# Differential attention on one core: a unit's two softmax halves joined in the next unit, its transpositions two units and its products with the values three units behind the scores

## The chip, the cores and the metric

The kernel runs on one NeuronCore of a Trainium2 chip, as one program. The metric is the time of one execution on the device, in microseconds. Matmuls run on TensorE (PE, with PEld for its weight loads), elementwise work on VectorE (DVE), ScalarE (ACT) and GpSimd (POOL), and every DMA is issued by SyncE (SP).

## The reference, cut to what matters

The program is a two-layer backbone over 1024 latent tokens and 256 context tokens of width 1024. Layer 0 mixes tokens by differential attention, layer 1 by a state-space scan; a dense block follows each. The change lies in the attention of layer 0, which computes, for each of 8 heads and each query, two softmaxes over the same keys and one product with the values:

```python
def attend(q, k, v):
    s = jnp.einsum('bqhcd,bkhcd->bhcqk', q, k).astype(jnp.float32)
    p = jax.nn.softmax(s, axis=-1)
    w = p[:, :, 0] - lam * p[:, :, 1]
    o = jnp.einsum('bhqk,bkhe->bqhe', w.astype(v.dtype), v)
    return rmsnorm(o, subln_g) * (1.0 - lambda_init)
```

Latent queries see 256 context and 1024 latent keys (1280), context queries only the 256 context keys. The arithmetic keeps float32 accuracy: an operand is split into a high and a low part, and a product is three matmuls (`mm3`, lines 130 to 134).

## The kernel before, in words

The stage in question is `phase_b` (lines 617 to 922). Its unit of work is a pair (head h, unit u). Unit 0 of a head takes all 256 context queries against 256 keys; units 1 to 8 take 128 latent queries each against 1280 keys. 8 heads of 9 units make 72 passes n of one loop (line 806), and five more passes drain what is left. Within `self.manual()` the instructions of PE, DVE, ACT and POOL stay in the order in which the loop writes them, each engine in its own queue; only SP's DMAs are placed by the scheduler.

What a unit goes through:

- *Scores* (`scores`, lines 507 to 520): twelve matmuls into five PSUM banks that every unit uses, so the next unit's scores wait until the maxima have read them.
- *Maxima* (`maxima`, 523 to 533): DVE copies each half c to SBUF (`p[0]` from a ring of two buffers, `p[1]` always the same buffer), negated extremum on the way; 1280 columns each, L533 (L529 in unit 0).
- *Exponentials* (`exps`, 535 to 544): ACT, one for each half, with their sums; L543 (L540 in unit 0).
- *Combine* (`combine`, 546 to 554): DVE joins the halves, half 0 minus lambda times half 1, in `p[0]`: a reciprocal (L551), a small product (L552) and one over 1280 columns (L554).
- *Transpositions* (`w_part`, 556 to 569): ten on PE, in three parts of four, two and four, into bank 5, the second half of bank 6, and bank 7 (bank 5 again where the unit has a projection).
- *Evacuation* (`w_evac`, 571 to 581) into `wT`, as a high and a low part: the first part by ACT (L574) and DVE (L575), the others by ACT (L579) and POOL (L580, L581).
- *Products with the values* (`values`, 651 to 656): two units make a pair of 256 queries (unit 0 is a pair of its own), 30 matmuls into the first half of bank 6, six for unit 0. Then `pair_out` (L662 on ACT, L663 on POOL) and one unit later `pair_sums` (L669 on PE, into the first columns of bank 6, and L670).

Before the change the transpositions of unit n - 1 stand in pass n, and the products of a pair two passes behind its last unit: for pairs that end in units 0, 2, 4, 6 and 8 that is in units 2, 4, 6, 8 and the next head's 1.

Beside this the loop projects keys and queries of the next head. `AHEAD` (line 588) says which projection belongs to which unit: two in unit 0 (the first, of 256 columns, ahead of the scores), one each in units 2, 3, 5 and 7; the others' matmuls (24 each) are cut into three fills that stand behind the three parts of the transpositions. A projection collects in bank 7. It is evacuated at the end of its unit by L466 (ACT) and L467 (DVE), or L461 and L462 for a block of 256 columns, and `next_post` brings its further steps, one in the middle and one at the end of each unit: L472 (POOL), L475 (DVE, in the middle), the split of the result by L137 (ACT) and L138 (DVE, at the end of units 0, 2, 4 and 7). Heads from 1 on also normalize the head before: `norm_calc` (675 to 677, DVE), `norm_rows` (a transposition, L684), and for each pair `norm_load` (two DMAs into one buffer) and `norm_pair` (L694 on DVE, which waits for them, then L137 and L138 on the tile W). In head 7 the projections are replaced by ten output products (`wo_group`), one in each pass from 65 on, and the drain normalizes head 7 itself (`norm7`).

A unit's pass queues, in this order: scores, maxima, products with the values, then the three parts. `late` is set where the pass has products with the values of a full pair; there the evacuation of the first two parts comes behind the exponentials, since it overwrites what the products read. Line 863 to 868 hold this order:

```python
                    if front and part < 2:
                        self.exps(u, part, p, sm, s0, sn)
                    if front and part == 1:
                        self.combine(u, p, s0, sn)
                    if late and part == 1:
                        evac()
```

At the end of the pass stand `pair_out`, `next_post`, the projection's evacuation, splits of weights, `norm_calc` or `norm_rows`, and `norm_pair`.

Of the kernel before, what the change touches and what calls it, by code (L numbers as in the profile page):

```python
# [6 lines left out]
F32 = mybir.dt.float32  # L7
F32R = mybir.dt.float32r
# [5 lines left out]
KB = 256  # L14
# [56 lines left out]
class Prog:  # L71
# [544 lines left out]

    def phase_b(self):
        nc, mm = self.nc, self.nc.tensor.matmul
        p0 = Ring([self.view(self.F1, 5 * i, (1280,)) for i in range(2)])
        p1 = self.view(self.F1, 10, (1280,))  # L620
        self.wraw = Ring([self.view(self.F1, 15 + 2 * i, (512,)) for i in range(3)])
        o = self.fv(6, 256)
        sq = self.adat
        self.raw = Ring([self.wv(0, 1024)])
# [64 lines left out]
        def norm_load(h, pair):  # L689
            self.dma(nob, self.od[h, :, 256 * pair : 256 * pair + 256])  # L690
            self.dma(nrb, self.rsd[h, 2 * pair : 2 * pair + 2].rearrange("a b -> (a b)").partition_broadcast(128))
# [54 lines left out]
        def wsplit6(j):  # L746
            hi, lo = wregs[j]
            self.split(hi, lo, wraw6[j], nc.gpsimd)
            wt6.extend((hi[:, i], lo[:, i]) for i in range(2))

        def beside7(u):

            if u == 0:
                self.oT = self.hgroups()
                nc.vector.memset(ones, 1.0)
            if u < 2:
                wsplit6(u + 1)
            for g, k0, k1 in {0: ((2, 0, 6),), 1: ((0, 0, 3),), 2: ((0, 3, 6),), 3: ((1, 0, 3),), 4: ((1, 3, 6),)}.get(u, ()):
                c0 = (256, 768, 0)[g]
                for k in range(k0, k1):  # L760
                    for j in range(2):
                        self.dma(self.oT[g][j][:, k].bitcast(F32), self.on[k, j, :, c0 : c0 + self.G_TOK[g]])
# [17 lines left out]
        wo_order = [8, 9] + list(range(8))  # L780
# [5 lines left out]
        load_q(0, 1)  # L786
        load_v(0)
        units = [(h, u) for h in range(8) for u in range(9)]
        prev, todo, sums, post, tail, run7 = None, [], [], [], [], []
        split = self.proj_weights(1, 1)  # L790
        split(0)
        wts = {1: split(1)}
# [10 lines left out]
                self.w_evac(*ready.pop(0))  # L803

        with self.manual():
            for n in range(72 + 5):
                h, u = units[n] if n < 72 else (8, 9)
                front = n < 72
                groups = []
                pv = todo.pop(0)[1:] if todo and todo[0][0] == n else None  # L810
                late = pv and pv[1]
                parts = 3 if prev and prev[1] else 1 if prev else 0
                if front and n - 6 >= 9 and (n - 6) % 9 < 5 and (n - 6) // 9 < 7:
                    norm_load((n - 6) // 9 - 1, (n - 6) % 9)
                if h == 7 and u > 5:
                    load6(u)
                if front:
                    K = loaded[h, 'k', 0], loaded[h, 'k', 1]
                    pair = (u + 1) // 2
                    Q = loaded[h, pair]  # L820
                    s0 = hst[:, 0, h]
                    p, sn, sm = (p0.next(), p1), self.stat.next(), self.stat.next()
                    if u == 5 and h < 7:
                        load_v(h + 1)
                        load_k(h + 1, 0)
                    if u % 2 == 0 and u < 8 and (h, pair + 1) not in loaded:
                        load_q(h, pair + 1)
                    if h < 7:
                        groups = [self.proj_group(h + 1, *a, wts[a[0]]) for a in self.AHEAD.get(u, ())]
                    if len(groups) == 2:  # L830
                        for f in groups[0][0] + groups[0][1]:
                            f()
                    self.scores(u, Q, K)
                    if u == 8 and h < 7:
                        load_k(h + 1, 1)
                        load_q(h + 1, 0)
                        load_q(h + 1, 1)
                    self.maxima(u, p, sm)
                if front:
                    if h < 7:  # L840
                        if u == 0:
                            qsplit = self.proj_weights(h + 1, 0)
                        if u == 5 and h < 6:
                            ksplit = self.proj_weights(h + 2, 1)
                if 65 <= n < 75:
                    groups = [wo_group(wo_order[n - 65])]
                fills = [[], [], []]
                if h >= 7 and groups:
                    fills = [groups[0][0][i : i + 2] for i in (0, 2, 4)]
                elif groups:  # L850
                    fills = [groups[-1][0][i:j] for i, j in (((0, 4), (4, 8), (8, 8)) if u == 3 else ((0, 3), (3, 6), (6, 8)))]
                if pv:
                    values(*pv)
                for part in range(3):
                    if part < parts:
                        tb = pb[:, 256:512] if part == 1 else self.bank(7 if part == 2 and not groups else 5)
                        t = self.w_part(prev[1], prev[2], part, tb)
                        ready.append((*t, part == 0))
                    if not late or part == 2:
                        evac()  # L860
                    if part == 1:
                        next_post()
                    if front and part < 2:
                        self.exps(u, part, p, sm, s0, sn)
                    if front and part == 1:
                        self.combine(u, p, s0, sn)
                    if late and part == 1:
                        evac()
                    if part == 0:
                        todo7, run7 = run7, []  # L870
                        for f in todo7:
                            f.pop(0)()
                            if f:
                                run7.append(f)
                    if part == (2 if n < 73 else 0):
                        while sums and sums[0][0] <= n:
                            sums.pop(0)[1]()
                    for f in fills[part]:
                        f()
                if pv:  # L880
                    pair_out(*pv)
                    sums.append((n + 1, lambda a=pv: pair_sums(*a)))
                    if pv[0] == 7:
                        tail.append((n + 1, pv[1]))
                next_post()
                if groups:
                    rest = groups[-1][1]
                    rest[0]()
                    post += rest[1:]
                if h < 7 and u in (0, 2):  # L890
                    wts[0] = qsplit(u // 2)
                if h < 6 and u in (6, 7):
                    wk = ksplit(u - 6)
                if u == 8 and h < 6:
                    wts[1] = wk
                if front and u % 2 == 0:
                    todo.append((n + 2, h, pair))
                prev = (h, u, p[0]) if front else None
                if 0 < h < 8:
                    if u == 3:  # L900
                        newton = norm_calc(h - 1)
                    elif u == 4:
                        newton()
                    elif u == 5:
                        norm_rows(h - 1)
                if h < 8 and n - 6 >= 9 and (n - 6) % 9 < 5 and (n - 6) // 9 < 7:
                    norm_pair((n - 6) // 9 - 1, (n - 6) % 9)
                if n == 72:
                    self.raw = Ring([self.wv(8, 1024), self.wv(12, 1024)])
                    self.wo_raws = [self.wo_load(3, 0), self.wo_load(0, 1)]  # L910
                if n == 60:
                    wload6(0)
                if n == 62:
                    wload6(1)
                    wload6(2)
                    wsplit6(0)
                if h == 7:
                    beside7(u)
                    if u > 5:
                        norm6(u)  # L920
                if tail and tail[0][0] == n:
                    run7.append(list(norm7(tail.pop(0)[1])))
# [1270 lines left out]
    def run(self):  # L2193
        tc = self.tc
        pool = lambda name, **kw: tc.tile_pool(name=name, bufs=1, **kw)
        with pool("cst") as self.cst, pool("psp", space=bass.MemoryType.PSUM) as psp, \
# [23 lines left out]
            with pool("r0") as rp, pool("fc") as cp:  # L2220
# [6 lines left out]
                    self.raw = Ring([self.wv(4 * i, 1024) for i in range(4)] + [self.f0(24.5 + 4 * i, 1024) for i in range(4)])  # L2227
                    self.phase_v()
                with pool("r1") as rp, pool("f1") as fp:
                    self.R1, self.F1 = rp.tile([128, 20 * KB], F32R, name="R1"), fp.tile([128, 21 * KB], F32, name="F1")  # L2230
                    self.phase_b()
                for g in range(3):
                    for j in range(2):
# [72 lines left out]
```

## Time and profile before

| What | Value |
|---|---|
| Times of three runs, us | 2940.19, 2940.97, 2946.08 (median 2940.97) |
| Span of the profiled execution, us (it has no separate time) | 2929.2 |
| PE busy | 2739.6 us, 94% of the span |
| DVE, ACT, POOL busy | 69%, 47%, 36% |
| Mean granted clock of TensorE | 0.980 |
| The 72 units and the drain | 237.55 to 926.80 us of the span |

How to read it: the busy time of an engine is the union of its instructions. A line such as L533 is one of `kernel.py`; a line in a helper (L132 to L134, L137, L138) serves many stages, so its tiles tell which one it is: `PS<-R` are products with the values, `PS<-H,R` projections. The arrow in `<-ACT F L579` names the instruction that ended a wait. Matmuls overlap in the profile: their pitch is shorter than their duration.

### The profile page before, as it was taken

What the parts mean: (1) busy time and instruction counts of PE and PEld (TensorE: products, weight loads), DVE (VectorE), ACT (ScalarE), POOL (GpSimd) and SP (SyncE); (2) the same over time, 40 slices, a digit from 0 to 9 for tenths busy, and PEclk for the clock granted to TensorE, in tenths of its full rate; (3) what the DMA queues carried; (4) which work ended last, traced back from release to release, by engine and by line L of the source; (5) the groups of instructions that cost most, each with busy time, mean ns of one, the idle gap of its engine ahead of it and who ended that gap; (6) DMA issues with size and microseconds to landing.
All of it is one profiled execution on the core that took longest, in us unless ns stands there. A gap on an engine that the chain in (4) does not pass through costs nothing.

```text
span 2929.2 us, 43646 instructions
## 1 busy us (share of the span) xinstructions
PE 2739.6 (94%) x15200; PEld 2287.5 (78%) x15200; DVE 2021.3 (69%) x2956; ACT 1367.5 (47%) x2555; POOL 1062.1 (36%) x923
## 2 busy tenths in 40 slices
PE   5998999999988999999999999688899899999999
PEld 3687888788777887878877778588788678878887
DVE  5355777777764477676688768699743687758566
ACT  3424555555553663333444435377543643345443
POOL 2213666666553700000020004499410543326324
PEclk8999999999989999999999999899999999999999
DMA  9956455555744448886699988468834254467544
GB/s 250 292 181 205 139 164 169 162 149 162 220 145 152 140 152 303 303 291 243 228 299 293 274 241 258 153 200 264 282 124 136 72 175 159 148 213 256 159 139 141
DMA packets 454122, 588.44 MB, mean 201 GB/s; under 512 B 62742, under 2 KB 299532, under 8 KB 450700
## 3 DMA queue, kind: packets, MB, share of 16 engines
q1 hardware_dynamic: 453900, 585.63, 63.6%
q8 instruction: 120, 1.97, 0.3%
q14 instruction: 102, 0.84, 0.1%
HBM read 398.48 MB, written 182.82 MB: 198 GB/s over the span
## 4 chain that ended last, share of the span: by engine, by line
PE 66%; DMA 12%; DVE 10%; issue 4%; ACT 4%; SPq 2%; POOL 2%; DVEq 0%; ACTq 0%; POOLq 0%
PE PS L132 19%; PE PS L133 18%; PE PS L134 18%; SPq L80 2%; PE PS L520 2%; PE PS L1797 2%; ACT F L543 2%; PE PS L1832 1%; PE PS L566 1%; DVE F L533 1%; DVE R L138 1%; DVE H L138 1%; PE PS L202 1%; DMA U<-in_mlp_w 1%; DMA U<-Aa 1%
## 5 line engine op out<-in xcount | busy, mean ns | idle before, releaser
L132 PE MATMUL PS<-H 128*128 128x512 f32 x1048 | 412.0, 395 | 7.7 <-DVE FD L1604 5.0
L133 PE MATMUL PS<-H 128*128 128x512 f32 x1048 | 410.4, 392 | 0.0
L134 PE MATMUL PS<-H 128*128 128x512 f32 x1048 | 409.8, 392 | 0.0
L132 PE MATMUL PS<-H,R 128*128 128x512 f32 (+1 forms) x836 | 311.2, 378 | 18.5 <-ACT F L579 13.7
L133 PE MATMUL PS<-H,R 128*128 128x512 f32 (+1 forms) x836 | 303.8, 363 | 1.1 <-POOL H L138 1.1
L134 PE MATMUL PS<-H,R 128*128 128x512 f32 (+1 forms) x836 | 303.6, 364 | 0.0
L137 ACT ACTIVATE R<-W 128x512 fp32r<-128x512 f32 (+1 forms) x203 | 142.9, 711 | 208.7 <-PE PS L133 114.9
L132 PEld LDWEIGHTS PS<-H 128*128 128x128 f32 x1048 | 197.9, 189 | 52.4 <-DVE FD L1604 5.3
L134 PEld LDWEIGHTS PS<-H 128*128 128x128 f32 x1048 | 197.7, 189 | 42.5 <-issue 1.0
L133 PEld LDWEIGHTS PS<-H 128*128 128x128 f32 x1048 | 197.9, 189 | 41.2 <-issue 1.2
L132 PE MATMUL PS<-R,H 128*128 128x512 f32 x532 | 214.7, 407 | 7.4 <-ACT H L137 6.0
L543 ACT ACTIVATE F<-F,stat 128x1280 f32<-128x1280 f32 x128 | 174.3, 1362 | 83.8 <-DVE F L533 83.5
L133 PE MATMUL PS<-R,H 128*128 128x512 f32 x532 | 210.8, 397 | 0.0
L134 PE MATMUL PS<-R,H 128*128 128x512 f32 x532 | 208.3, 395 | 0.0
L137 ACT ACTIVATE H<-U 128x640 fp32r<-128x640 f32 x216 | 132.8, 677 | 144.2 <-PE PS L133 110.7
L132 PEld LDWEIGHTS PS<-H,R 128*128 128x128 f32 x836 | 160.7, 193 | 47.6 <-ACT F L579 15.1
L138 DVE TENSOR_TENSOR H<-W,H 128x512 fp32r<-128x512 f32 (+1 forms) x137 | 128.6, 949 | 93.6 <-ACT H L137 93.6
L138 DVE TENSOR_TENSOR R<-W,R 128x512 fp32r<-128x512 f32 (+1 forms) x166 | 150.8, 915 | 60.8 <-ACT R L137 53.5
L533 DVE TENSOR_SCALAR_CACHE_REDUCE F<-PS 128x1280 f32<-128x1280 f32 x128 | 185.1, 1482 | 9.1 <-PE PS L520 8.9
L138 DVE TENSOR_TENSOR H<-U,H 128x640 fp32r<-128x640 f32 x216 | 163.4, 793 | 39.5 <-ACT H L137 39.3
L580 POOL TENSOR_SCALAR R<-F 128x256 fp32r<-128x256 f32 (+1 forms) x128 | 122.8, 959 | 172.1 <-ACT F L579 149.1
L134 PEld LDWEIGHTS PS<-H,R 128*128 128x128 f32 x836 | 160.7, 192 | 25.9 <-issue 0.8
(477 smaller groups left out, 6818.0 us busy)
## 6 DMA issues: line engine op xcount, KB each, us to landing
W<-in_mlp_w SPq DMA_DIRECT2D x184, 256.0 KB, 3.1
U<-Aa SPq DMA_DIRECT2D x108, 320.0 KB, 5.0
Aa<-FU SPq DMA_DIRECT2D x91, 320.0 KB, 4.6
Ad<-F SPq DMA_DIRECT2D x112, 256.0 KB, 3.2
W<-Ad SPq DMA_DIRECT2D x112, 256.0 KB, 2.8
W<-in_ada_w SPq DMA_DIRECT2D x32, 512.0 KB, 6.9
FU<-in_mlp_w SPq DMA_DIRECT2D x32, 512.0 KB, 6.3
Ta<-FU SPq DMA_DIRECT2D x16, 1024.0 KB, 5.6
```

Source lines behind the costliest of these rows:

```text
L80: return self.nc.sync.dma_start(out=out, in_=in_)
L132: mm(out, ah, bh, start=first, stop=False, **kw)
L133: mm(out, ah, bl, start=False, stop=False, **kw)
L134: mm(out, al, bh, start=False, stop=last, **kw)
L137: self.nc.scalar.activation(hi, src, AF.Copy)
L138: (lo_eng or self.nc.vector).tensor_tensor(lo, src, hi.bitcast(F32), ALU.subtract)
L202: self.nc.tensor.matmul(acc[32 * j : 32 * j + 32, 0:256], self.scT[:, 2 * k : 2 * k + 32], w[:, 256 * j : 256 * j + 256], start=k == 0, st ...
L520: mm(self.PS[:, 1280 * c + k0 : 1280 * c + k1], Q[:, c, r, qs], K[c][:, k0:k1], start=r == 0, stop=r == 1)
L533: ts(p[c], self.PS[:, 1280 * c : 1280 * c + 1280], 1.0, None, ALU.mult, ALU.min, accum_out=sm[:, c : c + 1])
L543: nc.scalar.activation(p[c], p[c], AF.Exp, bias=sm[:, c : c + 1], scale=-1.0, accum_out=sn[:, 0:1] if c else s0[:, u + 1 : u + 2])
L580: nc.gpsimd.tensor_scalar(hi, t, 1.0, 0.0, ALU.mult, ALU.add)
L1797: mm(b[:, o : o + 160], X[:, d, i, 64 * j : 64 * j + 128], U[:, 4 * n + i, cols], start=True, stop=True)
```

## The change: what it does

It moves three steps of a unit to a later pass of the loop and shifts what hangs on them:

- The combine of unit n is queued in pass n + 1, behind that pass's scores and ahead of its maxima. It was queued in pass n, behind the second exponential.
- The transpositions of unit n stand in pass n + 2 instead of n + 1 (`prevs` holds two units).
- The products with the values stand three passes behind the pair's last unit instead of two: in units 3, 5, 7 and the next head's 0 and 2.
- `p[0]` gets a third buffer, so the tile F1 grows from 21 to 26 KB per partition.
- `norm_load` and `norm_pair` come one pass later (units 7, 8, 0, 1, 2), `norm_calc` and its two followers in units 4, 5, 6 instead of 3, 4, 5 (in head 7 unchanged), the output products in passes 66 to 75, the weight splits in head 7 in units 0 and 2. The drain has six passes.

`AHEAD`, `late` and the banks are as before.

```diff
-        p0 = Ring([self.view(self.F1, 5 * i, (1280,)) for i in range(2)])
-        p1 = self.view(self.F1, 10, (1280,))
-        self.wraw = Ring([self.view(self.F1, 15 + 2 * i, (512,)) for i in range(3)])
+        p0 = Ring([self.view(self.F1, 5 * i, (1280,)) for i in range(3)])
+        p1 = self.view(self.F1, 15, (1280,))
+        self.wraw = Ring([self.view(self.F1, 20 + 2 * i, (512,)) for i in range(3)])
...
-            if u < 2:
-                wsplit6(u + 1)
+            if u in (0, 2):
+                wsplit6(u // 2 + 1)
...
-            for n in range(72 + 5):
+            for n in range(72 + 6):
                 h, u = units[n] if n < 72 else (8, 9)
+                prev = prevs.pop(0)
...
-                if front and n - 6 >= 9 and (n - 6) % 9 < 5 and (n - 6) // 9 < 7:
-                    norm_load((n - 6) // 9 - 1, (n - 6) % 9)
+                if front and n - 7 >= 9 and (n - 7) % 9 < 5 and (n - 7) // 9 < 7:
+                    norm_load((n - 7) // 9 - 1, (n - 7) % 9)
...
+                if joined:
+                    self.combine(*joined)
+                    joined = None
+                if front:
                     self.maxima(u, p, sm)
-                if front:
+                    joined = u, p, s0, sn
...
-                if 65 <= n < 75:
-                    groups = [wo_group(wo_order[n - 65])]
+                if 66 <= n < 76:
+                    groups = [wo_group(wo_order[n - 66])]
...
-                    if front and part == 1:
-                        self.combine(u, p, s0, sn)
...
-                    if part == (2 if n < 73 else 0):
+                    if part == (2 if n < 74 else 0):
...
-                    todo.append((n + 2, h, pair))
-                prev = (h, u, p[0]) if front else None
+                    todo.append((n + 3, h, pair))
+                prevs.append((h, u, p[0]) if front else None)
                 if 0 < h < 8:
-                    if u == 3:
+                    step = u - 3 - (h < 7)
+                    if step == 0:
                         newton = norm_calc(h - 1)
...
-                if h < 8 and n - 6 >= 9 and (n - 6) % 9 < 5 and (n - 6) // 9 < 7:
-                    norm_pair((n - 6) // 9 - 1, (n - 6) % 9)
+                if h < 8 and n - 7 >= 9 and (n - 7) % 9 < 5 and (n - 7) // 9 < 7:
+                    norm_pair((n - 7) // 9 - 1, (n - 7) % 9)
...
-                    self.R1, self.F1 = rp.tile([128, 20 * KB], F32R, name="R1"), fp.tile([128, 21 * KB], F32, name="F1")
+                    self.R1, self.F1 = rp.tile([128, 20 * KB], F32R, name="R1"), fp.tile([128, 26 * KB], F32, name="F1")
```

More of the change, by code (lines that the diff above doesn't have):

```diff
@@ L788, in phase_b @@
         units = [(h, u) for h in range(8) for u in range(9)]
-        prev, todo, sums, post, tail, run7 = None, [], [], [], [], []
+        prevs, joined, todo, sums, post, tail, run7 = [None, None], None, [], [], [], [], []
         split = self.proj_weights(1, 1)
@@ L896, in phase_b @@
                 if front and u % 2 == 0:
-                    todo.append((n + 2, h, pair))
-                prev = (h, u, p[0]) if front else None
+                    todo.append((n + 3, h, pair))
+                prevs.append((h, u, p[0]) if front else None)
                 if 0 < h < 8:
-                    if u == 3:
+                    step = u - 3 - (h < 7)
+                    if step == 0:
                         newton = norm_calc(h - 1)
-                    elif u == 4:
+                    elif step == 1:
                         newton()
-                    elif u == 5:
+                    elif step == 2:
                         norm_rows(h - 1)
-                if h < 8 and n - 6 >= 9 and (n - 6) % 9 < 5 and (n - 6) // 9 < 7:
-                    norm_pair((n - 6) // 9 - 1, (n - 6) % 9)
+                if h < 8 and n - 7 >= 9 and (n - 7) % 9 < 5 and (n - 7) // 9 < 7:
+                    norm_pair((n - 7) // 9 - 1, (n - 7) % 9)
                 if n == 72:
```

## The prediction

> **What bounds the kernel now.** I read the page first, then the busy time by stretches (one for each head, then one for each unit of a head), then who waited for whom, then pieces of the timeline. A row of stretches has start and end, length, busy time of PE, PEld, DVE, ACT and POOL with their counts, the granted clock, DMA share and GB/s.
>
> ```profile
> span 2929.2 us, 43646 instructions
> ```
> ```profile
> 237.55:312.75 75.20, 72.08 (x431) 62.91 (x432) 56.00 (x90) 43.07 (x82) 39.03 (x38) 0.96 0.50 158
> ...
> 724.61:803.88 79.27, 72.48 (x457) 63.39 (x455) 57.62 (x95) 41.27 (x86) 46.23 (x45) 1.00 0.72 220
> 803.88:926.80 122.92, 104.03 (x573) 88.03 (x573) 72.46 (x121) 60.38 (x119) 68.75 (x80) 0.93 0.41 133
> ```
> These are heads 0, 6 and 7 (7 with the drain). The change touches only this stage, 689 of the 2929 us, and PE is busy for most of it.
>
> ```profile
> 392.23:400.64 8.41, 8.41 (x48) 7.26 (x47) 5.23 (x18) 4.92 (x15) 4.33 (x7) 0.95 0.79 246
> 400.64:406.89 6.25, 6.25 (x48) 5.92 (x46) 5.78 (x7) 3.25 (x6) 3.23 (x3) 1.00 0.50 135
> 406.89:419.59 12.70, 10.67 (x59) 8.64 (x58) 8.41 (x14) 7.21 (x15) 5.83 (x6) 1.00 0.72 232
> 419.59:426.49 6.90, 6.90 (x51) 6.32 (x50) 5.88 (x8) 4.65 (x9) 5.65 (x6) 1.00 0.49 134
> 426.49:433.50 7.01, 7.01 (x54) 6.66 (x54) 6.66 (x12) 2.47 (x8) 4.63 (x4) 1.00 0.64 187
> 433.50:444.74 11.24, 9.72 (x54) 7.82 (x53) 9.06 (x14) 7.76 (x15) 8.75 (x9) 1.00 0.37 105
> 444.74:451.76 7.02, 7.02 (x54) 6.66 (x53) 5.17 (x9) 3.98 (x7) 2.50 (x2) 1.00 0.37 105
> 451.76:461.26 9.50, 9.50 (x54) 7.98 (x52) 8.91 (x12) 7.16 (x15) 8.66 (x10) 1.00 0.24 68
> 461.26:475.38 14.12, 11.62 (x78) 11.05 (x76) 9.94 (x13) 5.92 (x11) 10.57 (x11) 0.88 0.60 179
> ```
> Units 0 to 8 of head 2, each from its first score product to the next unit's. Heads 2 to 5 begin at 392.23 and end at 724.61: 332.38 / 4 = 83.1 each. Six units are full of matmuls; PE idles 2.0 in unit 2, 1.5 in unit 5 and 2.5 in unit 8. For heads 2 to 5 together that idle time is put down to:
>
> ```profile
> PE PS L132 <- ACT F L579: 10.1, 4, 2.6
> PE PS L566 <- DVE R L575: 8.4, 7, 1.5
> PE PS L133 <- DVE R L575: 5.4, 4, 1.5
> ```
> 23.9 us in four heads, 6.0 a head, by evacuations that come late. That is all the change can win in such a head, but for half-clock time behind the longest wait (below).
>
> **The change part by part.** First, what goes. DVE's combine (L551, L552, L554) waits for both exponentials of its own unit.
>
> ```profile
> L554 DVE SCALAR_TENSOR_TENSOR F<-F,stat 128x1280 f32<-128x1280 f32 x32 | 51.6, 1611 | 1.1
> ...
> L552 DVE SCALAR_TENSOR_TENSOR stat<-FC,stat,lamc 128x1 f32<-128x1 f32 x40 | 11.5, 287 | 1.4
> ...
> L551 DVE RECIPROCAL stat<-stat 128x1 f32<-128x1 f32 x40 | 6.5, 162 | 37.0 <-ACT F L543 32.8 <-ACT F L540 4.2
> ...
> L677 DVE SCALAR_TENSOR_TENSOR FC<-FC 128x10 f32<-128x10 f32 x4 | 4.6, 1147 | 0.1
> ```
> A combine is 1611 + 287 + 162 ns, about 2.0 us, and 37.0 / 4 = 9.2 us of DVE waiting a head end with the change. The L575 subtraction, which in units with products of the values now stands behind the combine, no longer does: its 13.8 us of PE waits, 3.5 a head, could go.
>
> Second, what moves on PE. The products with the values (30 matmuls at a pitch of 0.12, 3.6 us; 0.7 for the first pair) go one unit later. Before they lay in units 2 (the short one), 4, 6, 8 and the next head's 1; the projections lie in 0, 2, 3, 5 and 7, so only the 0.7 met one. Now the values lie in 3 (the short one), 5, 7, 0 and 2: each meets a projection, and units 1, 4, 6 and 8 have neither. From the rows above without their waits, with 3.6 us moved, about 0.5 for L669 (always one unit behind the values), 0.6 for the transpositions of the small unit 0, and 0.4 and 1.5 off for low clock in units 0 and 8, PE's work is 11.1, 3.8, 12.4, 7.6, 3.9, 12.6, 4.1, 12.6 and 6.8. Nothing is added, but a unit of 3.8 us is bounded no longer by PE but by its softmax.
>
> Third, the order on DVE. The combine of unit n now stands behind all that unit n queues at its end (L138, L467 or L462, L694, norm_calc) and ahead of the maxima of n + 1. Those items wait for ACT, PE or a DMA, and the time in which the combine ran is left idle.
>
> ```profile
> 460.35 1.66 DVE L554 SCALAR_TENSOR_TENSOR F<-F,stat 128x1280 f32<-128x1280 f32 x1
> 461.94 1.23 DVE L138 TENSOR_TENSOR R<-FC,R 128x512 fp32r<-128x512 f32 x1
> 463.27 0.69 DVE L467 SCALAR_TENSOR_TENSOR FC<-PS,W 128x512 f32<-128x512 f32 x1
> 463.88 1.42 DVE L694 SCALAR_TENSOR_TENSOR W<-W,lamc 128x256 f32<-128x256 f32 x1
> 465.23 1.48 DVE L533 TENSOR_SCALAR_CACHE_REDUCE F<-PS 128x1280 f32<-128x1280 f32 x1
> ```
> This is unit 7 into 8, whose scores start at 461.26. L467 reads the projection's bank, so it can't start before PE ends unit 7. The maxima, 3.97 behind the scores here, will follow L467 (0.7), L694 (1.4) and a combine (2.0), and L138 (1.2) too where ACT is late with it: 4.3 to 5.5, I take 5.0. In units 4 and 6, with neither L138 nor L694 ahead, it is 0.7 + 2.0 and an estimated 0.3 for the projection's last matmul: 3.0. Unit 1 has all of it: 5.1.
>
> ACT fixes the rest. In a unit without values its order is L574, exponential, L579, exponential, L579.
>
> ```profile
> 466.75 1.36 ACT L543 ACTIVATE F<-F,stat 128x1280 f32<-128x1280 f32 x1 [0.94 <-DVE F L533]
> ...
> 468.16 1.36 ACT L543 ACTIVATE F<-F,stat 128x1280 f32<-128x1280 f32 x1
> ...
> 469.52 0.57 ACT L574 ACTIVATE R<-PS 128x512 fp32r<-128x512 f32 x1
> 470.00 0.86 ACT L579 ACTIVATE F<-PS 128x256 f32<-128x256 f32 x2
> ```
> Counted from the maxima's start (465.23), the first exponential starts at +1.5 and the next thing at +3.0; the middle L579 then ends at +3.4, the second exponential at +4.9, the last L579 at +5.5. Two PE instructions wait for these two. L669 writes the bank that holds the middle transpositions until their L579; head 7 shows that wait in a unit without projection:
>
> ```profile
> 814.88 0.36 ACT L579 ACTIVATE F<-PS 128x256 f32<-128x256 f32 x1
> ```
> ```profile
> 815.39 0.77 PE L669 MATMUL PS<-lamc,adat 128*128 128x1 f32 x3 [3.57 <-ACT F L579]
> ```
> So a short unit lasts until its maxima's start + 3.5, and 0.6 for L669: unit 1 5.1 + 4.1 = 9.2 (work 3.8), unit 4 7.1 (3.9), unit 6 7.2 (4.1). The first projection of the next head needs bank 7, which the last transpositions of unit 8 hold until the last L579:
>
> ```profile
> 467.15 1.25 PE L566 MATMUL PS<-ident,F 128*128 128x128 f32 x10
> 470.91 0.39 PE L132 MATMUL PS<-H,R 128*128 128x256 f32 x1 [2.50 <-ACT F L579]
> 471.13 0.28 PE L133 MATMUL PS<-H,R 128*128 128x256 f32 x1
> 471.25 0.28 PE L134 MATMUL PS<-H,R 128*128 128x256 f32 x1
> ```
> (The last two starts are the pitch of 0.12.) PE now comes there 3.6 earlier and the maxima 1.0 later: a wait of 5.0 + 5.6 - 3.9 = 6.7 in place of 2.5, and with 24 matmuls at 0.12 unit 8 lasts 10.6 + 2.9 = 13.5.
>
> In unit 5 the last transpositions need bank 5, so L575, which with values in the unit follows both exponentials. Its maxima follow the combine of unit 4, behind L137 on ACT (0.6, as L574; done at the maxima of 4 + 6.4), L138 and norm_calc (1.6, with L677's 1.15, now in unit 4): the combine ends at +11.2, L575 at +16.8, where PE would come at +14.8. Between no wait and 2.0 I take 1.0: units 4 and 5 together 7.1 + 12.6 + 1.0 = 20.7. The same bank costs 0 to 2.2 in unit 3, by how long L694 waits for its DMA in unit 1; I take 1.1, so 8.7.
>
> Behind PE's idle time comes half clock:
>
> ```profile
> 471.00:475.00 4.00, 4.00 (x21) 4.00 (x22) 1.52 (x3) 0.13 (x1) 3.83 (x5) 0.57 0.61 209
> ```
> ```profile
> 544.97:557.60 12.63, 10.12 (x78) 9.55 (x76) 9.30 (x12) 5.92 (x11) 9.08 (x9) 1.00 0.58 164
> ```
> Behind the 2.5 us wait of head 2 the clock was 0.57 for 4 us and unit 8 lasted 14.12; in head 3 it stayed at 1.00 and unit 8 lasted 12.63. The price is 1.5; at 6.7 I charge it each time: unit 8 15.0. The Trainium skill ("TensorE: Matmul & The Clock Gate", section "Part 1: The HAM clock gate") has half rate come after an idle window of about 3.4 us; the trace had it at 2.5. By the page the 3 us waits of the other short units cost no clock and the 6.7 always does, so that it gives the same sum.
>
> The sum for each of heads 2 to 5: 11.1 + 9.2 + 12.4 + 8.7 + 20.7 + 7.2 + 12.6 + 15.0 = 96.9 against 83.1, **+13.8**. For heads 1 to 5 +69. Head 0 has neither L694 nor norm_calc, and no transpositions in its first two units: I take half, +7. Head 6 has no projection behind unit 8, only the short units: +11. In head 7 one of ten output products moves from idle time in unit 2 into the drain, while norm_load's round trips pace its first units as before: between -4 and +4, I take +1. The 5 KB more of F1 lie in the same pool and cost nothing. Total **+88**. The page gives the execution's span, 2929.2, and no time of its own; the median of the runs, 2940.97, is 11.8 above it, which I take as what lies around the span. 2941 + 88 = **3029**.
>
> Fixed are L467 or L462 and the combine ahead of the maxima: with these alone (unit 1 7.1, unit 3 7.6, 4 and 5 19.7, unit 8 11.5) a head takes 89.2, +6.1, the whole +39: 2980. With all upper ends and two more half clocks a head takes 102.9, the whole +131: 3072.
>
> **The rivals.** *Only the fixed terms*: 2980, chance 0.15. For it: DVE idles 18 us of 83 a head and may have done L138 and L694 early. Against: L138 needs ACT behind its unit's last L579. *The waits simply go*: with the softmax a unit ahead L575 is never late, and the L579 wait stays as it is. Over the stage that is
>
> ```profile
> PE PS L566 <- DVE R L575: 19.4, 13, 4.3
> ...
> PE PS L133 <- DVE R L575: 9.7, 6, 3.1
> ```
> 29.1 us: **2912**, chance 0.09. It decides if the maxima of units 1, 4, 6 and 8 start within 1.6 of the scores, where a head comes to its 83 again; L467 speaks against it. *A wash, or the engines don't follow the program's order*: 2941, 0.04; the DVE rows above do follow it. *Worse*, half clock behind every wait: 3072 and over, 0.04. My forecast: 0.68.
>
> The range 2970 to 3065 holds the forecast and the fixed-terms case. About 0.2%, 6 us, is what a measurement can tell from no change. Slower 0.68 + 0.15 + 0.04 = 0.87, within 0.04, faster 0.09.
>
> **What would show it.** Right: PE waits on L579 before L669 in units 1, 4 and 6; 5 to 7 us before the first projection behind unit 8; maxima 3 to 5 us behind the scores in short units; no DVE wait for L543 at L551; a clock under 1 behind unit 8. Wrong: short units of 4 us, or maxima close behind their scores in them.

## The result, and the profile after

The changed kernel takes **3109.51 us** (median of 4 runs, 3102.55 to 3112.29), the kernel before 2940.58 beside it: a ratio of **1.0575** [1.0554, 1.0597], 169 us slower. The forecast was +88 and its range ended at 3065: the sign was right, the size about half. (A run's time is about 2 us above its own span: the profiled run of the change took 3112.29, with a span of 3110.2.)

The page after, its first lines and the clock in 40 slices:

```profile
span 3110.2 us, 43672 instructions
...
PE 2812.2 (90%) x15200; PEld 2352.4 (76%) x15200; DVE 2038.3 (66%) x2956; ACT 1370.8 (44%) x2555; POOL 1055.9 (34%) x923
...
PEclk8998888888888999999999999989999999999999
```

The number of matmuls is as before, yet PE is busy 73 us longer. The clock row (the share of full speed granted to TensorE, in tenths) shows where: slices 4 to 13, 233 to 1011 us, all read 8. By stretches, after: heads 0 and 1, heads 2 to 5 together, head 6, head 7 with the drain (columns as in the prediction).

```profile
239.69:335.78 96.09, 77.42 (x390) 66.78 (x391) 56.92 (x86) 41.65 (x78) 33.73 (x35) 0.84 0.41 128
335.78:442.22 106.44, 85.38 (x482) 75.50 (x481) 64.76 (x98) 46.51 (x92) 46.70 (x48) 0.87 0.34 102
442.22:872.12 429.90, 342.20 (x1918) 302.71 (x1917) 267.92 (x404) 190.12 (x380) 204.07 (x205) 0.87 0.43 124
872.12:972.41 100.29, 79.34 (x457) 69.65 (x456) 65.34 (x100) 45.15 (x89) 44.15 (x45) 0.90 0.61 190
972.41:1097.10 124.69, 106.91 (x615) 91.58 (x615) 74.46 (x120) 58.78 (x120) 73.76 (x84) 0.92 0.38 121
```

And heads 2 to 5 before, in one row:

```profile
392.23:724.61 332.38, 306.60 (x1918) 270.48 (x1917) 259.10 (x404) 189.75 (x381) 214.75 (x205) 0.98 0.55 160
```

The stage lasts 857.4 us instead of 689.3, +168.2, and nearly all of the loss lies in it. (The two profiled spans differ by 181.0; the other 12.9 are within what the runs of the kernel before differ by, 2928 to 2950 over all rounds.) Heads 0 and 1 lose 20.9 and 27.0, heads 2 to 5 24.4 each, head 6 21.0, head 7 1.8. The row of heads 2 to 5 splits its 24.4. Length less PE busy is 21.9 us a head after and 6.4 before: **15.5 us more waiting**. PE's busy time is 85.6 a head against 76.7, for the same 1918 matmuls: **8.9 us more for the same work**. The clock of 0.87 says why: a mean of 0.87 between 1 and 0.5 is 26% of the time at half clock, 28 us of a head; 0.98 before was 3. (That the clock reads either 1 or 0.5 is seen where it is read piece by piece, in the last section.)

Who PE waits for, in the stage:

```profile
PE PS L669 <- ACT F L579: 134.0, 28, 10.4
PE PS L566 <- DVE R L575: 12.7, 10, 1.7
```

One wait has replaced the three of before: the row sums (L669), three times in head 0, four times in each of heads 1 to 6 and once in head 7, wait for ACT's evacuation of the middle transpositions. Unit by unit, head 4 after:

```profile
657.10:668.28 11.18, 11.18 (x75) 10.08 (x73) 4.94 (x14) 4.59 (x14) 1.61 (x3) 1.00 0.53 165
668.28:678.49 10.21, 4.46 (x28) 3.80 (x26) 8.94 (x14) 4.93 (x9) 5.40 (x7) 0.90 0.51 142
678.49:692.52 14.03, 14.03 (x71) 12.30 (x72) 8.48 (x11) 5.58 (x12) 6.02 (x6) 0.83 0.57 154
692.52:701.74 9.22, 7.55 (x57) 7.01 (x56) 7.40 (x10) 5.03 (x9) 4.22 (x4) 1.00 0.66 218
701.74:710.15 8.41, 4.11 (x29) 3.49 (x28) 7.04 (x10) 4.18 (x11) 5.50 (x7) 1.00 0.42 116
710.15:724.34 14.19, 14.19 (x78) 12.40 (x78) 8.00 (x13) 6.32 (x13) 4.91 (x6) 0.88 0.30 75
724.34:733.38 9.04, 4.69 (x28) 3.98 (x27) 6.95 (x12) 5.08 (x10) 5.32 (x7) 0.87 0.35 102
733.38:748.04 14.66, 14.66 (x77) 12.75 (x77) 5.52 (x7) 5.55 (x11) 7.08 (x7) 0.85 0.04 10
748.04:764.36 16.32, 9.87 (x51) 9.14 (x50) 9.78 (x12) 6.25 (x13) 10.83 (x11) 0.71 0.62 176
```

PE idles 4.3 to 6.5 us in units 1, 4, 6 and 8, which have neither a projection of their own nor products with the values. Each full unit behind such a one (2, 5, 7) runs at a mean clock of 0.83 to 0.88.

Unit 1 of that head, as DVE, ACT and PE lived it (start, duration, instruction, idle time before):

```profile
668.55 1.82 DVE L138 TENSOR_TENSOR R<-FC,R 128x512 fp32r<-128x512 f32 x1 [4.65 <-ACT R L137]
670.48 0.69 DVE L467 SCALAR_TENSOR_TENSOR FC<-PS,W 128x512 f32<-128x512 f32 x1
671.09 1.27 DVE L694 SCALAR_TENSOR_TENSOR W<-W,lamc 128x256 f32<-128x256 f32 x1
672.28 0.15 DVE L551 RECIPROCAL stat<-stat 128x1 f32<-128x1 f32 x1
...
674.25 1.48 DVE L533 TENSOR_SCALAR_CACHE_REDUCE F<-PS 128x1280 f32<-128x1280 f32 x1
```
```profile
675.77 1.36 ACT L543 ACTIVATE F<-F,stat 128x1280 f32<-128x1280 f32 x1 [2.43 <-DVE F L533]
...
677.13 0.36 ACT L579 ACTIVATE F<-PS 128x256 f32<-128x256 f32 x1
```
```profile
670.61 1.27 PE L566 MATMUL PS<-ident,F 128*128 128x128 f32 x10
677.64 0.98 PE L669 MATMUL PS<-lamc,adat 128*128 128x1 f32 x4 [5.75 <-ACT F L579]
```

PE has all ten transpositions behind it by 671.9. DVE does L138, L467, L694 and the combine before the maxima, which start 5.97 after the scores; ACT waits for them with the exponential, and the small evacuation that PE needs stands behind that. It ends 3.2 after the maxima's start, and PE begins again at 3.4.

### The profile page after: what moved, and what is told of

Read it like the earlier page. It is cut to its first block, busy times and chain, and to the rows that moved or that the text cites. A ratio compares the mean times of both kernels' runs of the same rounds, so it can differ in the third digit from the quotient of the medians.

```text
span 3110.2 us, 43672 instructions
## 1 busy us (share of the span) xinstructions
PE 2812.2 (90%) x15200; PEld 2352.4 (76%) x15200; DVE 2038.3 (66%) x2956; ACT 1370.8 (44%) x2555; POOL 1055.9 (34%) x923
## 4 chain that ended last, share of the span: by engine, by line
PE 53%; DVE 6%; DMA 6%; issue 3%; POOL 2%; ACT 1%; SPq 1%; DVEq 0%; POOLq 0%; ACTq 0%
PE PS L132 16%; PE PS L134 16%; PE PS L133 16%; PE PS L1801 2%; PE PS L1836 1%; DVE H L138 1%; PE PS L520 1%; SPq L80 1%; DMA K<-in_mlp_w 1%; DVE FD L1819 1%; DMA FU<-in_mlp_w 1%; DMA U<-tbd 1%; DVE FD L1810 1%; DMA recd<-U 0%; PE PS L202 0%
## 5 line engine op out<-in xcount | busy, mean ns | idle before, releaser
L132 PE MATMUL PS<-H 128*128 128x512 f32 x1048 | 412.4, 395 | 6.1 <-DVE FD L1608 3.8
L132 PE MATMUL PS<-H,R 128*128 128x512 f32 (+1 forms) x836 | 312.7, 379 | 5.5 <-ACT FC L670 4.5
L132 PEld LDWEIGHTS PS<-H 128*128 128x128 f32 x1048 | 198.2, 189 | 51.0 <-DVE FD L1608 4.1
L132 PE MATMUL PS<-R,H 128*128 128x512 f32 x532 | 214.3, 406 | 5.2 <-ACT H L137 3.6
L520 PE MATMUL PS<-R,R 128*128 128x512 f32 x720 | 195.5, 432 | 3.3 <-DVE F L533 3.3
L138 DVE TENSOR_TENSOR R<-W,R 128x512 fp32r<-128x512 f32 (+1 forms) x166 | 149.6, 910 | 65.6 <-ACT R L137 58.4
L580 POOL TENSOR_SCALAR R<-F 128x256 fp32r<-128x256 f32 (+1 forms) x128 | 79.5, 621 | 327.7 <-ACT F L579 306.3
L138 DVE TENSOR_TENSOR H<-U,H 128x640 fp32r<-128x640 f32 x216 | 163.4, 793 | 41.2 <-ACT H L137 41.0
L138 DVE TENSOR_TENSOR H<-W,H 128x512 fp32r<-128x512 f32 (+1 forms) x137 | 128.3, 947 | 93.1 <-ACT H L137 91.9
L132 PEld LDWEIGHTS PS<-H,R 128*128 128x128 f32 x836 | 163.7, 196 | 32.3 <-issue 4.1
```

Source lines behind the costliest of these rows:

```text
L132: mm(out, ah, bh, start=first, stop=False, **kw)
L138: (lo_eng or self.nc.vector).tensor_tensor(lo, src, hi.bitcast(F32), ALU.subtract)
L520: mm(self.PS[:, 1280 * c + k0 : 1280 * c + k1], Q[:, c, r, qs], K[c][:, k0:k1], start=r == 0, stop=r == 1)
L580: nc.gpsimd.tensor_scalar(hi, t, 1.0, 0.0, ALU.mult, ALU.add)
```

## The experiments

**Mine**: the waits come from ACT's order (L579 behind an exponential, which waits for maxima that the combine has delayed), and half clock follows them. **Against it**: that one moved part alone costs the whole, or that the time lies in PE's own work and its clock.

### The parts alone

*Combine back in its own unit, the rest of the change kept* (the opposite edit, on the kernel before, moves only the combine):

```diff
-                if joined:
-                    self.combine(*joined)
-                    joined = None
...
+                    if front and part == 1:
+                        self.combine(u, p, s0, sn)
```

> The changed kernel with the combine alone put back into its own unit; transpositions stay two units and products with the values three units behind. Theory: the cost has three parts, units that have neither a projection nor products with the values (1, 4, 6, 8), which last as long as their softmax; the combine, which stands between the end of a projection and the next maxima and makes those units about 2 us longer; and half clock behind the waits. Then four units a head get 2 us and more shorter, with about 3 us less half clock: 11 us a head, 3030 us (3000 to 3060). Rival 1, the place of the combine is all of it: 2941. Rival 2, the place of the combine doesn't matter: 3110.

Measured 3025.77, 1.0302 [1.0272, 1.0331]: as expected. L669 waits 77.5 us instead of 134.0, for ACT still and now in part for POOL:

```profile
PE PS L669 <- ACT F L579: 62.3, 21, 4.1
PE PS L669 <- POOL FC L472: 15.2, 7, 2.6
```

So the moved transpositions and products alone cost 89 us: units 1, 4, 6 and 8 make PE wait even with the maxima as early as before (4.0, 2.4, 1.6 and 4.0 us behind the scores in head 4).

*Only the combine moved, on the kernel before:*

> The kernel before with the combine alone moved into the next unit, ahead of its maxima; transpositions one unit and values two units behind as before. Theory: the values keep their places in units without projections, so no unit becomes empty; the transpositions of units 0, 3 and 5 now wait 2 to 3 us each for a combine that stands behind L138, L467 and L462, against 3 us of L575 waits won: about 5 us a head slower, 2980 us (2955 to 3005). Rival 1, the combine's place is the whole cost: 3110. What the edit would give if the waits simply went: 2912.

Measured **3096.5**, 1.0547 [1.0509, 1.0584]: a miss for my theory. PE's largest wait, then the place in DVE's and in PE's queue:

```profile
PE PS L566 <- DVE F L554: 118.8, 36, 8.1
```
```profile
707.53 0.69 DVE L575 TENSOR_TENSOR R<-PS,R 128x512 fp32r<-128x512 f32 x1 [1.40 <-ACT R L574]
709.08 1.11 DVE L138 TENSOR_TENSOR R<-FC,R 128x512 fp32r<-128x512 f32 x1 [0.86 <-ACT R L137]
...
711.36 1.87 DVE L554 SCALAR_TENSOR_TENSOR F<-F,stat 128x1280 f32<-128x1280 f32 x1
```
```profile
713.28 1.11 PE L566 MATMUL PS<-ident,F 128*128 128x128 f32 x4 [6.03 <-DVE F L554]
```

With the transpositions one unit behind, they read what the combine has just made, and the combine stands behind a split of the last unit: PE waits for it directly. In the changed kernel they read a combine one unit older, so this wait isn't there. The parts don't add: 159 and 89 alone, each against the kernel before in its own round, 169 together.

*One pass more* (transpositions three, products four units behind, four buffers for `p[0]`), and on top of it the combine in its own unit behind the three parts. In both, one weight split of head 7 overwrites values that the last pair of head 6 still reads, so that pair's product differs; their times are read here for the order of the queues alone.

```diff
-            for n in range(72 + 6):
+            for n in range(72 + 7):
...
-                    todo.append((n + 3, h, pair))
+                    todo.append((n + 4, h, pair))
```

The second, on top of the first (the joined lines at the maxima go out):

```diff
                         f()
+                if front:
+                    self.combine(u, p, s0, sn)
```

> The changed kernel with transpositions three and products with the values four units behind the scores (a fourth buffer of p[0], normalization one unit later). The values then stand in units 4 (the short one), 6, 8, 1 and 3: all but the last again in units without a projection. The combine stays in the next unit. Theory: empty units are one half of the cost, and the transpositions, which waited for the combine when it alone was moved, have two units of slack; only unit 4 (4.6 us of work) and the wait behind unit 8 remain: about 86 us a head, 2961 us (2930 to 3000). Rival 1, the combine behind the end items sets the loop by itself, as it did alone (3096): 3080 or more. Rival 2, a longer pipeline is the cost: above 3110.

> e5 with the combine in its own unit, behind the evacuations of the three parts and ahead of L138, L467 and L694. Theory: the maxima then follow the scores by 3.9 us in unit 8 and 1.7 in unit 4, L575 isn't behind a combine, and no transposition waits for one: about 80 us a head, 2920 us (2895 to 2945), faster than both kernels. Rival, the combine's place doesn't matter once no unit is empty: equal to e5.

Measured 2996.41, 1.0197 [1.0177, 1.0218], and 2968.41, 1.01 [1.0083, 1.0118]. The first lies at the upper end of the expected range, and the rivals fall: an even longer distance is *faster* than the change. Three of the four full pairs' products now lie in units 6, 8 and 1, which have no projection. PE's largest wait is a quarter of what it was, though it is the same one:

```profile
PE PS L669 <- ACT F L579: 34.7, 8, 5.6
```

The second is 28 faster than the first but stays 30 above before, where I had expected a gain. Together, medians in us, by how far the transpositions and the products stand behind the scores:

| Units behind | Combine in its own unit | Combine in the next unit |
|---|---|---|
| 1 and 2 | 2941 (before) | 3097 |
| 2 and 3 | 3026 | 3110 (the change) |
| 3 and 4 | 2968 (behind the parts) | 2996 |

### ACT's order

*Row sums ahead of the unit's transpositions:* L669 and L670 are queued right behind the products with the values.

```diff
+                if front:
+                    while sums and sums[0][0] <= n:
+                        sums.pop(0)[1]()
                 for part in range(3):
```

> The changed kernel with the row sums (L669, L670) queued ahead of the transpositions of their unit instead of behind them, so that L669 no longer waits for the middle evacuation L579. Theory: L669 is only the first of several that wait for the same softmax: behind it the next scores wait for the maxima (unit 1 gets 2.8 us shorter, unit 4 2.4), L684 waits for the same L579 in unit 6, the first projection waits for the last L579 in unit 8: 5 us a head and some half clock, 3060 us (3035 to 3085). Rival, the L669 wait (134 us in the trace) is a cost by itself: about 2975.

Measured 3063.03, 1.0435 [1.0398, 1.0472]: expected. L669 no longer waits for L579, and the next instructions on PE inherit the wait:

```profile
PE PS L132 <- ACT F L579: 33.7, 6, 6.1
PE PS L520 <- DVE F L533: 23.8, 20, 3.1
```

*Evacuations first:* in units that have neither a projection nor products with the values, all transpositions, their evacuations and the row sums stand ahead of the exponentials.

```diff
+                if front and not late and not groups:
+                    for part in range(parts):
...
+                        evac()
+                    parts = 0
+                    while sums and sums[0][0] <= n:
+                        sums.pop(0)[1]()
```

> The changed kernel; in units with neither a projection nor values, all transpositions, their evacuations and the row sums are queued ahead of the unit's exponentials on every engine. Theory: what binds these units is that L579 stands behind the exponentials on ACT, though its transpositions are done 2 to 3 us before the maxima start; with the evacuations first L669, L684 and the first projection wait for nothing, and the units last until the next scores get their banks from the maxima: 7.4, 6.0, 5.0 and 8.0 us for units 1, 4, 6, 8 instead of 10.2, 8.4, 9.0, 16.3; unit 5 gets a wait for L575 of 3. About 89 us a head for 107.5: 2985 us (2955 to 3015). Rival, DVE's chain with the combine binds them whatever ACT does: above 3050.

Measured **3001.1**, 1.0217 [1.0189, 1.0245], within the range expected: 108 of the 169 us go with ACT's order alone (DVE, POOL and PE keep theirs in these units), the combine staying in the next unit. Heads 2 to 5, then the stage's two largest waits:

```profile
410.67:783.00 372.33, 322.01 (x1918) 278.24 (x1917) 259.89 (x405) 192.64 (x383) 201.03 (x206) 0.96 0.50 145
```
```profile
PE PS L669 <- ACT F L579: 28.5, 28, 2.7
PE PS L520 <- DVE F L533: 27.0, 29, 3.1
```

The 28 waits are still there, but 1.0 long in place of 4.8; behind them PE now waits for the maxima itself. PE's work fell too, from 85.6 to 80.5 a head, with the clock at 0.96.

*The same with the combine back in its own unit*, behind the exponentials (the edit of the first experiment), then behind the late evacuations:

```diff
-                    if front and part == 1:
-                        self.combine(u, p, s0, sn)
...
+                if front:
+                    self.combine(u, p, s0, sn)
```

> e8 with the combine back in its own unit, so what is left of the change is transpositions and values one unit later. Theory: both binds are gone; maxima follow the scores by 2 to 4 us, units 1, 4, 6 and 8 last 5.5, 4.1, 4.2 and 7.2, units 5 and 0 keep some wait for L575: about 79 us a head, 2910 us (2890 to 2945), faster than before. Rival, what is late next (L575 behind the combine in units 5, 7, 0, 2, or values waiting for POOL) takes it back: 2960 to 2990.

> e9 with the combine behind the late evacuations of its own unit instead of ahead of them. Theory: L575 in units 5, 7, 0 and 2 comes 2 us earlier, the next maxima at most 0.7 later: 2905 us (2885 to 2940). Rival, as in the kernel before with the same edit (2960 against 2938): slower than e9 by 10 to 20.

Measured 2982.1, 1.0146 [1.0123, 1.0168], and 2955.47, 1.0054 [1.0034, 1.0074]. Both were expected below the kernel before, and neither is. The first is the rival's case: PE now waits for L575, which stands behind the combine. The second lies outside its range too; it is 27 us faster than the first, where 5 were expected.

```profile
PE PS L566 <- DVE R L575: 32.3, 17, 2.9
```
```profile
PE PS L566 <- DVE R L575: 14.2, 13, 1.5
```

### The half clock

*PE kept busy:* useless matmuls of 512 columns into bank 7, ahead of the last transpositions in units 1, 4, 6 and 8 (20, 12, 12 and 20 of them) of heads 1 to 6, on the changed kernel.

```diff
+        IDLE = {1: 20, 4: 12, 6: 12, 8: 20}
...
+                    if part == 2 and front and n > 9 and h < 7 and u in IDLE:
+                        for _ in range(IDLE[u]):
+                            mm(self.bank(7), K[1][:, 0:128], K[1][:, 0:512], start=True, stop=True)
```

> The changed kernel with matmuls of no use (their bank is written over by the transpositions behind them) in the waits of heads 1 to 6: 20, 12, 12 and 20 of 512 columns ahead of the last transpositions in units 1, 4, 6 and 8. They shorten no wait and take nothing from another engine. Theory: a head of 107.4 us has 21.9 us of waits and 85.5 of work that took 76.7 before; the 9 us between are half clock behind the waits, and go if PE is kept busy in them: 6 heads by 9 us, 3055 us (3035 to 3075), granted clock about 0.98 in these heads. Rival, the clock is a sign and not a cost, since DVE's chain sets the head's length: 3110 or more.

The first version, which read a query tile, took 3143.08 (1.0701 [1.0669, 1.0733]). In unit 8 that tile is being reloaded and the useless matmuls wait for its DMA, a fault of the experiment:

```profile
PE PS L863 <- DMA R<-Qd: 74.9, 6, 13.1
```

In head 4, units 2 and 7 were 2 us shorter in it. With keys as operands:

> As e4_kept_busy, but the matmuls of no use read a key buffer that is not loaded again in that unit; in e4 their operand was a query buffer whose next load they had to wait for in unit 8 (74.9 us in its trace). Where that didn't stand in the way, units 2 and 7 behind the filled units 1 and 6 were 2.1 and 2.0 us shorter in e4. Theory: half clock behind the waits costs about 9 us a head in the changed kernel; with the waits filled 6 heads get 6 to 9 us shorter: 3065 us (3050 to 3080). Rival, the clock is no cost: 3110.

Measured **3071.26**, 1.0458 [1.0433, 1.0484]: 38 us less than the change although PE does 256 more matmuls in heads 2 to 5.

```profile
432.31:842.23 409.92, 375.00 (x2174) 326.99 (x2173) 268.45 (x405) 189.57 (x381) 204.83 (x206) 0.96 0.45 131
```

The clock is back at 0.96, and a head takes 102.5 instead of 107.5: the half clock that went was worth at least 5.0 us a head, taking it that the useless matmuls save nothing in any other way.

### The gain that wasn't there

*The combine behind the late evacuations, in the kernel before* (the edit just shown): L575 no longer stands behind it, so the prediction's 3.5 us a head of L575 waits could go.

> The kernel before with the combine moved by a few instructions only: behind the late evacuations of its own unit (L575), still ahead of L138, L467 and L694. Theory: what the change wanted to win is the 3.5 us a head in which PE waits for an L575 behind the combine; this wins them without an empty unit and without a combine behind the end items: 2915 us (2905 to 2930). Rival, what is late next takes it back (the next transpositions or maxima, since the combine ends 0.7 us later): 2941.

Measured 2960.17, 1.0078 [1.0057, 1.0098]: slower. The mechanism is the rival's, and it took back more than the rival's 2941.

```profile
PE PS L566 <- DVE F L554: 42.9, 24, 3.2
```

PE's waits for L575, 30.8 us before (21.1 and 9.7), are down to 1.9. The L575 wait was the combine's shadow. With L575 ahead, the next unit's transpositions wait for the combine itself, and longer.

*The last evacuation between the exponentials of unit 8, in the kernel before*, with all three parts of the transpositions queued ahead:

```diff
+                last = u == 8 and h < 6 and late and not groups
...
+                    if last and part == 1:
+                        self.w_evac(*ready.pop(2))
```

> The kernel before with one edit in unit 8: the last transpositions' L579 is queued on ACT between the two exponentials instead of behind both and behind L574 and the middle L579. Theory, from what bound the changed kernel (an evacuation that PE needs stands behind exponentials that PE doesn't need): the first projection behind unit 8 starts about 1.8 us earlier in 6 heads, the half clock that followed that wait in three of them goes, the second exponential and the combine come 0.6 later, which nothing waits for: 2925 us (2915 to 2935). Rival, the later exponential is handed on to the next unit's maxima: 2939.

Measured 2934.73 (12 runs), 0.9991 [0.9973, 1.0009]: no difference is shown. The wait on L579 before the first projection is handed to the projection behind it, which waits for the first one's evacuation (L462). Before, then with the edit:

```profile
PE PS L132 <- ACT F L579: 13.7, 6, 2.6
PE PS L132 <- DVE R L462: 1.6, 2, 0.8
```
```profile
PE PS L132 <- ACT F L579: 4.4, 6, 0.9
PE PS L132 <- DVE R L462: 11.9, 6, 3.2
```

No version measurably beat the kernel before.

## Why the prediction was right in sign and short in size

**What bounds.** Right: PE, only this stage, and little to win. The 3.5 us a head of L575 waits were not won by any order tried. The 11.8 us between the span and the median were read wrongly: a run lies about 2 us above its own span, so the profiled execution was merely a fast one. The forecast starts from the median, and its +88 doesn't hang on this.

**The waits.** Right within a tenth in their sum, in part by luck. The unit sums of the forecast hold 20.5 us of waits a head (5.4 in unit 1, 1.1 in 3, 4.2 in 4 and 5, 3.1 in 6, 6.7 in 8); 21.9 were measured. Unit 1's maxima came 5.97 behind the scores (forecast 5.1; L138 took 1.82 and not 1.2), and PE went on 3.4 later (forecast 3.5). The wait of unit 8 stands before L669, and not before L132; it was 5.70 in head 4, for 6.7. In unit 4 of that head the maxima came 4.58 behind the scores (forecast 3.0), and PE idled 4.3 for 3.2; unit 6 idled 4.35 for 3.1. Unit 5, with 1.0 forecast, had no wait of its own, which makes up for 1.0 of those 2.4.

**The half clock** is the step that failed, a term of the sum that was mis-sized. "Behind PE's idle time comes half clock", the prediction says, with a price of 1.5, charged once a head, behind unit 8; the other short units were to cost none. Measured were 8.9 us a head by the rows of heads 2 to 5, of which the kept-busy run gave back 5.0. Two things were off. It came behind all four waits, not one: in head 4 units 2, 5 and 7 lasted 14.0, 14.2 and 14.7 (forecast 12.4, 12.6 + 1.0 of wait, 12.6) with no idle time in them. And each time cost more. Unit 8 of head 4, from the first projection on:

```profile
759.10:764.40 5.30, 5.30 (x25) 5.30 (x26) 0.84 (x1) 0.42 (x1) 4.01 (x4) 0.50 0.76 235
```

24 matmuls at a pitch of 0.21 instead of 0.12 are 2.2 us, not 1.5. The Trainium skill ("TensorE: Matmul & The Clock Gate", section "Part 1: The HAM clock gate") has half rate after an idle window of about 3.4 us and full rate only after a busy one. I took from the first half that waits of about 3 us are free, and passed over the forecast's own 5.4 in unit 1, which by the same reading had to be charged; so the rule did not give the same sum. The wait in unit 4 then became 4.3, that before L669 in unit 6 3.4, and shorter ones brought half clock too (last section).

**The heads.** Of the 81 us missed, heads 2 to 5 hold 42, head 0 14, head 1 13 and head 6 10. Heads 2 to 5 took 107.5 each and not 96.9: 1.4 of the miss lies in the waits, 9.2 in PE's work, 85.6 against the 76.4 that the forecast's units hold without their waits. Head 0 was charged half, for want of L694 and norm_calc. It waits nearly as the others do (18.7 against 3.1 before, from its rows) and paid 20.9 for 7, although 41 of its matmuls went to a later head: L694 isn't what makes most of the waits. Head 6, +21.0 for +11, got 14.2 more of waits and 6.9 of work. Head 7, +1.8 for +1, was right.

**The rivals.** "Only the fixed terms" (2980) and "the waits simply go" (2912) are out. "Worse, half clock behind every wait" is what happened, and had 0.04; its 102.9 a head was short as well, because it counted three half clocks at 1.5 each. The range failed with that price: an effect that follows each idle time should have been priced four times for the upper end.

**What stays open.** Little of the 8.9 us. The kept-busy run gave back 5.0, with 20 of 28 us of half clock; its useless matmuls also delay the last transpositions. The trace of the change puts nearly all of it down to the clock: in heads 2 to 5 PE was busy for 89.8 us while the clock read 0.50 (18 stretches, 116.0 us in all), and for 10.2 before (three stretches). That is 19.9 more a head, and at pitches of 0.21 and 0.43 (matmuls of 256 and 512 columns) instead of 0.12 and 0.23 it loses an estimated 8.5 to 9.3 us.

```profile
sum 116.03, PE 89.80 PEld 80.44 DVE 71.20 ACT 52.24 POOL 77.86; mean PE 4.99 PEld 4.47 DVE 3.96 ACT 2.90 POOL 4.33
```

It isn't settled why the versions with the waits mostly gone still stop 15 to 30 us above before.

## What to carry to other kernels

When idle time is put in front of TensorE, charge it and the half clock behind it, each time: here waits of 1.7 to 5.8 us brought half clock, the shorter ones not every time, and 15.5 us more of waiting a head brought 8.9 us more of work. Before a step is moved later to take it off one engine's path, look at which in-order queue its successor stands in; here evacuations of 0.4 and 0.6 us queued behind exponentials carried 108 of 169 us. A wait that a profile names may be the shadow of another: the L575 wait vanished when the combine was moved out of its way, and a longer one stood in its place.

## What the runs showed that I had not expected

A wait well under 3.4 us also brings half clock. In the changed kernel, PE's row sums in unit 4 of head 3, then the clock of the stretch behind the wait:

```profile
601.46 0.99 PE L669 MATMUL PS<-lamc,adat 128*128 128x1 f32 x4 [2.73 <-ACT F L579]
```
```profile
601.28:608.11 6.83, 6.65 (x23) 5.90 (x24) 5.28 (x10) 2.45 (x6) 3.72 (x4) 0.50 0.30 79
```

Behind 2.73 us of waiting the clock is 0.50 for 6.8 us. The profile before already held a shorter one, in unit 2 of head 3, which lasted 14.0 us for the 12.7 of head 2:

```profile
494.45 0.38 PE L133 MATMUL PS<-R 128*128 128x256 f32 x1 [1.50 <-DVE R L575]
```
```profile
495.42:498.83 3.41, 3.41 (x12) 2.73 (x10) 2.08 (x4) 1.05 (x3) 0.82 (x2) 0.50 0.96 361
```

What decides is where the wait falls. In both traces the clock is 1.00 or 0.50 and nothing else. In the 72 units and the drain, every stretch of half clock lasts 3.41 us or a multiple of it (6.83 behind most waits of the change), and within each trace all start whole multiples of 3.41 us apart, on one grid. In both kernels each piece of this grid at full clock in which PE idled 1.9 us or more was followed by half clock, and none with under 1.5; the few between went either way. So the 2.5 us before the first projection brought half clock in head 2 of the kernel before and not in head 3, where a boundary of the grid at 553.4 us cut them into 1.3 and 1.2.
